# First stage of a two-request encoder layer: the sample's modulation products and the rotary tables moved from GpSimd to VectorE

## The chip, the cores and the metric

The kernel runs on one core of a Trainium2 chip. The core has five engines that work side by side, each through its own instruction stream in a fixed order: TensorE (PE in the profile, with its weight loads as PEld), VectorE (DVE), ScalarE (ACT), GpSimd (POOL) and SyncE (SP), which here issues most of the DMA transfers. The engines wait for each other through semaphores. The metric is the device time of one execution in microseconds (us); lower is better. The profile is that of one execution.

## The reference, cut to what matters

One encoder layer is applied to two requests that share all weights: a prompt of 512 tokens and a sample of 1,024 tokens, each with 1,024 channels, in float32. For each of them:

```
mod = (silu(c) @ w_ada + b_ada)             # 6 x 1024: shift, scale, gate for mixer and MLP
h   = rmsnorm(x, g_pre_mix) * (1 + scale_a) + shift_a
q, k, v, u = split(h @ w_in)                # 512 + 128 + 128 + 512 columns
q, k = rope(rmsnorm(q, g_q)), rope(rmsnorm(k, g_k))
a   = attention(q, k, v)                    # 8 heads, 2 key/value heads, bidirectional
p   = multiscale_pool(u)                    # 4 groups, windows 2, 4, 8, 16
x   = x + gate_a * rmsnorm(concat(a, p) @ w_out, g_post_mix)
h   = rmsnorm(x, g_pre_mlp) * (1 + scale_m) + shift_m
x   = x + gate_m * rmsnorm(relu(h @ w_ff1)**2 @ w_ff2, g_post_mlp)
```

The change concerns the first two lines, `mod` and `h`, and the tables of the rotary embedding `rope`: cosines and sines, multiplied by the gains g_q and g_k. `silu(c)` is one vector of 1,024 numbers for each request, so `mod` is a matrix-vector product with a matrix of 1,024 by 6,144. Two of its six parts, shift_a and scale_a, have to be there before the first projection `h @ w_in` can begin.

## The kernel before, in words

Activations lie transposed: channels on the 128 partitions in eight blocks, tokens along the free dimension. The weights w_ada come as 48 tiles of 128 output channels by 1,024 inputs, 512 KB each. A product of such a tile with silu(c), which `make_cb` has spread over all partitions (`cb0` for the prompt, `cb1` for the sample), summed along the free dimension, gives 128 numbers of `mod`. `gemv_part` (L224) does product and sum in one VectorE instruction (L225) and writes the sum into a column of `mod`. `mod_mix` (L228) then adds the bias (L231) and forms (1 + scale) times the norm's gain (L232) for one block of 128 channels.

The first stage is `in_proj_p` (L479). It loads the prompt's eight blocks of x (`hp`), sums their squares (L495 to L499) and turns them into a reciprocal root for each token by `norm_vec` (small VectorE steps at L164 to L168, then PE at L177 and ACT at L180). Then comes a loop over eight blocks k of channels (L509). Each turn
- loads two tiles of w_ada, `jb = k` for the shift and `jb = 8 + k` for the scale, into a ring of seven buffers (tag `ga`, L512 and L513), and computes the prompt's part of both on VectorE (L515);
- loads the block's weights `w`, which have a buffer for each k (L519, L520);
- calls `mod_mix(0, k)`, scales hp[k] by the root on VectorE (L522), and applies scale and shift on ScalarE (L523);
- runs seven matmuls that add block k into seven PSUM banks (L526). The profile counts two matmuls for each of these;
- computes the sample's part of the same two tiles. For k below 6 the product is done by GpSimd (L530) and the sum by ScalarE one turn later (`sums_late`, L503 to L507, called at L524 behind the turn's L523). For k = 6 and 7 both are one instruction on VectorE (L533, which is L225 in the profile).

A w_ada tile is free for the next load once the sample's part has read it. After the loop the PSUM banks are copied out and three more blocks of the projection are computed with the same input (L545 to L557). The sample's `mod_mix(1, k)` is called in the next stage, by `make_h` (L351 to L353).

`setup_rest` (L297) loads edge_t, wp, the gains `gt` and the cosines and sines `cs`, scales one half of the gains on VectorE (L302), and forms the rotary tables `tabs` with ten GpSimd operations on 128 by 256 elements (L311 to L315). It is called in one go after 20 steps of `in_proj_p` (L1224). A step is one `yield`, one of the seven matmuls; so this point lies near the end of turn k = 2. From there `weave` (L26) runs the rest of `in_proj_p` and, at 0.32 steps to each of its steps, `pre_norm` (L322): eight loads of the sample's x (512 KB each, L327, two buffers), ScalarE's squares (L328), and the sample's norm.

The order of each engine's stream is set by a scheduler that follows the order in which the program names the instructions, but may put one that is ready earlier. Waits for a buffer stay in the stream: an engine, or SP's queue, that meets such a wait stands still with all that is behind it. `tc.keep_in_program_order(ins)` pins an instruction behind the one named just before it on the same engine.

Of the kernel before, what the change touches and what calls it, by code (L numbers as in the profile page):

```python
# [11 lines left out]
AF = mybir.ActivationFunctionType  # L12
AL = mybir.AluOpType
# [12 lines left out]
def weave(fg, bgs):  # L26

    credit = [0.0] * len(bgs)
    for _ in fg:
        for i, (bg, rate) in enumerate(bgs):  # L30
            credit[i] += rate
            while credit[i] >= 1.0:
                credit[i] -= 1.0
                next(bg, None)
# [7 lines left out]
def chain(*gs):  # L42
    for g in gs:
        yield from g
# [3 lines left out]
def hymba_encoder_layer(ctx, tc, xp, xs, ns_, vec, gqk, rope, edge, ident_in, w_ada_c,  # L48
                        w_in_k, w_in, w_pool, w_out, w_ff1, w_ff2, yp, ys):
    nc = tc.nc  # L50
# [51 lines left out]
    mod = const.tile([128, 48, 2], F32, name="mod")  # L102
# [121 lines left out]
    def gemv_part(c, jb, r, cb, out):  # L224
        return nc.vector.tensor_tensor_reduce(out=out, in0=r, in1=cb, op0=AL.mult, op1=AL.add,  # L225
                                              scale=1.0, scalar=0.0, accum_out=mod[:, jb, c:c + 1])
# [65 lines left out]
    tabs = inp.tile([128, 4, 8, 64], F32, name="tabs")  # L292
# [4 lines left out]
    def setup_rest():  # L297
        dma(edge_t, edge)
        dma(wp.rearrange("p g d -> p (g d)"), w_pool)
        gt = tmp("gt", "y")  # L300
        dma(gt[:, 0:128], gqk.partition_broadcast(128))
        nc.vector.tensor_scalar(gt[:, 0:64], gt[:, 0:64], 0.125, None, op0=AL.mult)  # L302
        cst = tmp("cs", "t2")
        dma(cst, rope)
        cs = cst.rearrange("p (a b d) -> p a b d", a=2, b=8)

        def gb(lo):
            return gt[:, lo:lo + 32].unsqueeze(1).to_broadcast([128, 8, 32])
        for qk in range(2):
            o = 64 * qk  # L310
            nc.gpsimd.tensor_tensor(tabs[:, 2 * qk, :, 0:32], cs[:, 0], gb(o), AL.mult)  # L311
            nc.gpsimd.tensor_tensor(tabs[:, 2 * qk, :, 32:64], cs[:, 0], gb(o + 32), AL.mult)
            nc.gpsimd.tensor_scalar(tabs[:, 2 * qk + 1, :, 0:32], cs[:, 1], -1.0, None, op0=AL.mult)
            nc.gpsimd.tensor_tensor(tabs[:, 2 * qk + 1, :, 0:32], tabs[:, 2 * qk + 1, :, 0:32], gb(o + 32), AL.mult)
            nc.gpsimd.tensor_tensor(tabs[:, 2 * qk + 1, :, 32:64], cs[:, 1], gb(o), AL.mult)  # L315

    R_t = {}
    h_t = {}
# [108 lines left out]
    def u_evac(ps, g):  # L427
        u = pq.tile([128, 8 + 512 + 8], F32, name=f"up{g}")
        nc.gpsimd.memset(u[:, 0:8], 0.0)
        nc.gpsimd.memset(u[:, 520:528], 0.0)  # L430
        u_t[g] = u
        nc.scalar.activation(out=u[:, 8:520], in_=ps, func=AF.Copy)
# [46 lines left out]
    def in_proj_p():  # L479


        make_cb(0, cb0, ps_t, "t")
        make_cb(1, cb1, ps_t, "t")
        pss = [mm_tile() for _ in range(2)]
        pss += [ps_t.tile([128, 512], F32, tag="t", name="tb") for _ in range(2)]
        pss += [s2[:, 0:512], s2[:, 512:1024], ps_x.tile([128, 512], F32, tag="x", name="xb")]
        hp = []
        ss = st_p.tile([128, 512], F32, tag="ss", name="ss")
        for k in range(KB):
            t = pd.tile([128, 512], F32, name=f"hp{k}")  # L490
            dma(t, xp[k])
            hp.append(t)
        for k in range(KB):
            if k == 0:
                nc.scalar.activation(out=ss, in_=hp[k], func=AF.Square)  # L495
            else:
                sq = st_p.tile([128, 512], F32, tag="sq", name="sq")
                nc.scalar.activation(out=sq, in_=hp[k], func=AF.Square)
                nc.vector.tensor_tensor(ss, ss, sq, AL.add)  # L499
        R = norm_vec([ss])  # L500
        late = []

        def sums_late():  # L503
            while late:
                jb, r = late.pop(0)
                tc.keep_in_program_order(
                    nc.scalar.activation(out=r, in_=r, func=AF.Copy, accum_out=mod[:, jb, 1:2]))  # L507

        for k in range(KB):  # L509
            g = []  # L510
            for jb in (k, 8 + k):
                r = pa.tile([128, 1024], F32, tag="ga", name="ga", bufs=7)  # L512
                dma(r, w_ada_c[jb])  # L513
                junk = inp.tile([128, 1024], BF16, tag="j", name="junk", bufs=1)
                ins = gemv_part(0, jb, r, cb0, junk)  # L515
                if k:
                    tc.keep_in_program_order(ins)
                g.append((jb, r))
            w = pb[k].tile([128, 7, 128], F32, name=f"pw{k}")  # L519
            dma(w.rearrange("p b m -> p (b m)"), w_in_k[k])  # L520
            mod_mix(0, k)
            nc.vector.tensor_tensor(hp[k], hp[k], R, AL.mult)  # L522
            nc.scalar.activation(out=hp[k], in_=hp[k], func=AF.Identity, bias=mod[:, k, 0:1], scale=a_mix[:, k, 0:1])  # L523
            sums_late()  # L524
            for i in range(7):
                nc.tensor.matmul(pss[i], lhsT=w[:, i, :], rhs=hp[k], start=(k == 0), stop=(k == KB - 1))  # L526
                yield
            for jb, r in g:
                if k < 6:
                    nc.gpsimd.tensor_tensor(r, r, cb1, AL.mult)  # L530
                    late.append((jb, r))
                else:
                    tc.keep_in_program_order(gemv_part(1, jb, r, cb1, r))  # L533
        sums_late()
        xs_ = {}
        for i in (2, 3, 0, 4, 5, 1):
            xs_[STRIPES[i]] = evac(pss[i], pq.tile([128, 512], F32, name=f"xp{i}"))
        u_evac(pss[6], 0)
        yield
        posts.append(qk_post(0, 0, xs_[4], 4))  # L540
        posts.append(qk_post(0, 0, xs_[0], 0))
        posts.append(v_post(0, 0, xs_[5]))
        posts.append(u_post(0, 0))
        rp = run_posts()
        for g in range(1, 4):  # L545
            w = pc[3 - g].tile([128, 8, 128], F32, name=f"pu{g}")
            dma(w, w_in[6 + g].rearrange("p k m -> p (k m)"))
            ps = mm_tile()
            for k in range(KB):
                nc.tensor.matmul(ps, lhsT=w[:, k, :], rhs=hp[k], start=(k == 0), stop=(k == KB - 1))  # L550
                if k % 2:
                    next(rp, None)
                yield
            u_evac(ps, g)
            posts.append(u_post(0, g))
        for b in (1, 2, 3):
            posts.append(qk_post(0, 0, xs_[b], b))  # L557
        rest.append(rp)
# [661 lines left out]
    cb1 = pa.tile([128, 1024], F32, name="cb1")  # L1220
    ip = in_proj_p()
    for _ in range(20):
        next(ip)
    setup_rest()  # L1224
    weave(ip, [(chain(pre_norm(0), pre_norm(1)), 0.32)])
    for z in (pb_close, pa_close, pc_close, pd_close):
        z()

# [205 lines left out]
```

## Time and profile before

| | |
|---|---|
| time, median of 3 runs | 1739.14 us (1735.07 to 1743.35) |
| the profiled execution | 1736.51 us, of which the span from first to last instruction is 1734.7 |
| PE busy | 1627.4 us, 94% of the span |
| DVE busy | 1279.3 us, 74% |
| ACT busy | 892.2 us, 51% |
| POOL busy | 153.2 us, 9% |
| chain that ended last | PE 70%, DVE 12%, DMA 10%, ACT 4% |
| mean granted PE clock | 0.976 |

Durations and times of start count from the first instruction. In the views, a line `L225 DVE ... out<-in x16` names the line of the code, the engine, the tile written and the tiles read, and the number of instructions. Square brackets behind an instruction give the engine's idle time just before it and what ended it. A row of the waits reads: engine and instruction that waited, `<-` what it waited for, then total us, times and the longest. `SPq` is SP's queue of DMA issues; the length of an entry there includes its wait for a buffer.

The stage in question runs from about 5 us, when the first tile of w_ada is issued, to about 96 us, when PE goes on to the remaining blocks of the prompt's projection.

### The profile page before, as it was taken

Reading aid. Unit: us, or ns where it says so; the run is one execution under the profiler, and the core shown is the slowest. Engines: PE = TensorE matmul, PEld = TensorE weight load, DVE = VectorE, ACT = ScalarE, POOL = GpSimd, SP = SyncE. Lnnn points to the kernel's source line nnn. Section 1 sums busy time; section 2 is a strip of 40 time slices with the busy share of each in tenths; the row PEclk is TensorE's granted clock in tenths of the full one; section 3 lists DMA queues with packets and bytes.
Section 4 is the critical chain, followed back from the end, with each engine's and each line's share of the span. In section 5 each row is a group of like instructions: output and inputs, shape, how many; then the busy total and the mean of one; then the engine's idle time right before and its main releaser. Section 6 shows DMA issues by size and latency. Waiting matters only on the chain.

```text
span 1734.7 us, 21886 instructions
## 1 busy us (share of the span) xinstructions
PE 1627.4 (94%) x7676; PEld 1303.1 (75%) x7676; DVE 1279.3 (74%) x2151; ACT 892.2 (51%) x1444; POOL 153.2 (9%) x127
## 2 busy tenths in 40 slices
PE   6798999889998999999998999999999989999995
PEld 3357887678887888888886677788888768888875
DVE  7797887878766786666645577888876476868767
ACT  3465655468655555555433456744445554444432
POOL 4501000201100100101012200000000000000014
PEclk7899999999999999999998999999999999999997
DMA  6555566833555453332334766566653656344324
GB/s 235 206 194 171 152 188 216 258 96 108 184 168 169 161 178 122 98 113 86 95 100 143 231 215 213 171 242 218 227 210 127 213 180 194 128 146 142 109 77 146
DMA packets 150110, 287.44 MB, mean 166 GB/s; under 512 B 14960, under 2 KB 56176, under 8 KB 150000
## 3 DMA queue, kind: packets, MB, share of 16 engines
q1 hardware_dynamic: 125552, 258.25, 45.8%
q10 hardware_dynamic: 24448, 27.80, 5.2%
q8 instruction: 61, 1.00, 0.2%
q14 instruction: 49, 0.40, 0.1%
HBM read 223.07 MB, written 61.34 MB: 164 GB/s over the span
## 4 chain that ended last, share of the span: by engine, by line
PE 70%; DVE 12%; DMA 10%; ACT 4%; issue 3%; POOL 1%; SPq 1%; DVEq 0%; POOLq 0%; ACTq 0%
PE pa L834 17%; PE mm L834 9%; PE mm L157 8%; PE mm L156 8%; PE mm L155 8%; PE pc L834 5%; DMA raw<-in_w_ada_c 4%; PE s L612 3%; PE pT L631 3%; PE x L645 2%; PE x L644 2%; DMA raw<-in_w_ff 2%; DVE wl L136 1%; DVE raw L225 1%; DVE junk L225 1%
## 5 line engine op out<-in xcount | busy, mean ns | idle before, releaser
L155 PE MATMUL mm<-fh,wh 128*128 128x512 f32 x448 | 185.0, 414 | 11.1 <-ACT fh L708 8.3
L156 PE MATMUL mm<-fl,wh 128*128 128x512 f32 x448 | 180.4, 404 | 2.8 <-DVE fl L709 2.8
L157 PE MATMUL mm<-fh,wl 128*128 128x512 f32 x448 | 179.3, 401 | 0.9 <-DVE wl L136 0.9
L135 ACT ACTIVATE wh<-raw 128x1024 fp32r<-128x1024 f32 (+2 forms) x106 | 105.2, 994 | 119.8 <-PE mm L156 82.5
L136 DVE TENSOR_TENSOR wl<-raw,wh 128x1024 fp32r<-128x1024 f32 (+2 forms) x106 | 125.2, 1182 | 51.6 <-ACT wh L135 51.5
L834 PE MATMUL pa<-fo,wh 128*128 128x512 f32 x448 | 138.9, 391 | 0.7 <-ACT x L970 0.7
L635 DVE TENSOR_TENSOR pl<-pT,ph 128x512 fp32r<-128x512 f32 x160 | 108.2, 685 | 26.5 <-ACT ph L634 25.7
L619 ACT ACTIVATE p<-s,amx 128x1024 f32<-128x1024 f32 (+1 forms) x96 | 93.1, 970 | 59.6 <-DVE amx L617 55.5
L617 DVE TENSOR_REDUCE amx<-s 128x1 f32<-128x1024 f32 (+1 forms) x96 | 100.0, 1041 | 31.4 <-PE s L612 30.9
L634 ACT ACTIVATE ph<-pT 128x512 fp32r<-128x512 f32 x160 | 94.2, 594 | 38.9 <-PE pT L631 33.2
L834 PE MATMUL mm<-fo,wh 128*128 128x512 f32 x336 | 106.2, 398 | 4.0 <-ACT wh L840 4.0
L155 PEld LDWEIGHTS mm<-fh,wh 128*128 128x128 f32 x448 | 85.5, 192 | 29.8 <-ACT fh L708 10.1
L155 PE MATMUL mm<-hA,wh 128*128 128x512 f32 x256 | 106.0, 415 | 0.0
L156 PEld LDWEIGHTS mm<-fl,wh 128*128 128x128 f32 x448 | 86.1, 192 | 22.8 <-DVE fl L709 6.0
L631 PE MATMUL pT<-ident,p 128*128 128x128 f32 x640 | 95.4, 273 | 7.6 <-ACT p L622 3.5
L157 PEld LDWEIGHTS mm<-fh,wl 128*128 128x128 f32 x448 | 86.0, 192 | 21.0 <-DVE wl L136 1.8
L157 PE MATMUL mm<-hA,wl 128*128 128x512 f32 x256 | 100.6, 393 | 0.0
L156 PE MATMUL mm<-hA,wh 128*128 128x512 f32 x256 | 100.5, 393 | 0.0
L612 PE MATMUL s<-kst,q 128*128 128x512 f32 x320 | 92.3, 402 | 7.8 <-ACT p L619 4.3
L631 PEld LDWEIGHTS pT<-ident,p 128*128 128x128 f32 x640 | 77.6, 140 | 28.6 <-ACT p L622 6.1
L834 PEld LDWEIGHTS pa<-fo,wh 128*128 128x128 f32 x448 | 84.0, 188 | 19.5 <-ACT x L970 1.1
L834 PE MATMUL pa<-fo,wl 128*128 128x512 f32 x224 | 87.6, 391 | 0.0
(288 smaller groups left out, 3918.0 us busy)
## 6 DMA issues: line engine op xcount, KB each, us to landing
raw<-in_w_ff SPq DMA_DIRECT2D x56, 512.0 KB, 3.8
f_d<-x SPq DMA_DIRECT2D x98, 256.0 KB, 2.9
raw<-f_d SPq DMA_DIRECT2D x98, 256.0 KB, 3.0
raw<-in_w_ada_c SPq DMA_DIRECT2D x40, 512.0 KB, 4.0
g<-in_w_ada_c SPq DMA_DIRECT2D x24, 512.0 KB, 4.3
q<-q_d SPq DMA_DIRECT2D x96, 128.0 KB, 3.2
raw<-in_w_out SPq DMA_DIRECT2D x24, 512.0 KB, 4.4
rawx<-in_w_ff SPq DMA_DIRECT2D x20, 512.0 KB, 4.0
```

What stands on the lines that cost most here:

```text
L135: nc.scalar.activation(out=fh, in_=r[:, :n], func=AF.Copy)
L136: nc.vector.tensor_tensor(fl, r[:, :n], fh.bitcast(F32), AL.subtract)
L155: nc.tensor.matmul(ps, lhsT=wh[:, k, :], rhs=ah, start=(i == 0), stop=False)
L156: nc.tensor.matmul(ps, lhsT=wh[:, k, :], rhs=al, start=False, stop=False)
L157: nc.tensor.matmul(ps, lhsT=wl[:, k, :], rhs=ah, start=False, stop=(i == len(ks) - 1))
L612: nc.tensor.matmul(s[:, f * 512:(f + 1) * 512], lhsT=q[:, h, p, :], rhs=kst[c][:, kv, f * 512:(f + 1) * 512].bitcast(F32R), start=(p == 0) ...
L617: nc.vector.tensor_reduce(mx, s[:, :n], AX.X, AL.max, negate=True)
L619: nc.scalar.activation(out=pr, in_=s[:, :n], func=AF.Exp, bias=mx, accum_out=den)
L631: nc.tensor.transpose(t[:, k, :], pr[:, (4 * f + k) * 128:(4 * f + k + 1) * 128], ident)
L634: nc.scalar.activation(out=hi, in_=t, func=AF.Copy)
L635: nc.vector.tensor_tensor(lo, t, hi.bitcast(F32), AL.subtract)
L834: nc.tensor.matmul(ps, lhsT=x[:, k, :], rhs=y, start=start and k == i == 0, stop=k == n - 1 and i == 2, skip_group_check=not start)
```

## The change

The sample's products in the first stage are all done by `gemv_part` on VectorE, product and sum in one instruction. `late` now holds the tiles whose sample part is still to do, and `sample_part(4)`, called behind the turn's L523, works it down to four tiles: in turn k the two tiles of block k - 2. The last four follow after the loop with `sample_part(0)`, behind the copies out of PSUM. The GpSimd products and ScalarE's sums are gone from this stage. All sample parts are pinned.

`setup_rest` becomes a generator that is woven in at 0.13 steps for each step of `in_proj_p`, in three pieces: the loads and the scaling of `gt` (after 8 further steps, so at the end of turn 3), the four table operations for q (after 16), and the four for k (after 24). They run on VectorE, and the two GpSimd steps for the negated sine are one instruction now.

```diff
--- before.py
+++ after.py
@@ -306,13 +306,15 @@
 
         def gb(lo):
             return gt[:, lo:lo + 32].unsqueeze(1).to_broadcast([128, 8, 32])
+        yield
         for qk in range(2):
             o = 64 * qk
-            nc.gpsimd.tensor_tensor(tabs[:, 2 * qk, :, 0:32], cs[:, 0], gb(o), AL.mult)
-            nc.gpsimd.tensor_tensor(tabs[:, 2 * qk, :, 32:64], cs[:, 0], gb(o + 32), AL.mult)
-            nc.gpsimd.tensor_scalar(tabs[:, 2 * qk + 1, :, 0:32], cs[:, 1], -1.0, None, op0=AL.mult)
-            nc.gpsimd.tensor_tensor(tabs[:, 2 * qk + 1, :, 0:32], tabs[:, 2 * qk + 1, :, 0:32], gb(o + 32), AL.mult)
-            nc.gpsimd.tensor_tensor(tabs[:, 2 * qk + 1, :, 32:64], cs[:, 1], gb(o), AL.mult)
+            nc.vector.tensor_tensor(tabs[:, 2 * qk, :, 0:32], cs[:, 0], gb(o), AL.mult)
+            nc.vector.tensor_tensor(tabs[:, 2 * qk, :, 32:64], cs[:, 0], gb(o + 32), AL.mult)
+            nc.vector.scalar_tensor_tensor(tabs[:, 2 * qk + 1, :, 0:32], cs[:, 1], -1.0, gb(o + 32),
+                                           op0=AL.mult, op1=AL.mult)
+            nc.vector.tensor_tensor(tabs[:, 2 * qk + 1, :, 32:64], cs[:, 1], gb(o), AL.mult)
+            yield
 
     R_t = {}
     h_t = {}
@@ -500,14 +502,13 @@
         R = norm_vec([ss])
         late = []
 
-        def sums_late():
-            while late:
+        def sample_part(lag):
+
+            while len(late) > lag:
                 jb, r = late.pop(0)
-                tc.keep_in_program_order(
-                    nc.scalar.activation(out=r, in_=r, func=AF.Copy, accum_out=mod[:, jb, 1:2]))
+                tc.keep_in_program_order(gemv_part(1, jb, r, cb1, r))
 
         for k in range(KB):
-            g = []
             for jb in (k, 8 + k):
                 r = pa.tile([128, 1024], F32, tag="ga", name="ga", bufs=7)
                 dma(r, w_ada_c[jb])
@@ -515,27 +516,21 @@
                 ins = gemv_part(0, jb, r, cb0, junk)
                 if k:
                     tc.keep_in_program_order(ins)
-                g.append((jb, r))
+                late.append((jb, r))
             w = pb[k].tile([128, 7, 128], F32, name=f"pw{k}")
             dma(w.rearrange("p b m -> p (b m)"), w_in_k[k])
             mod_mix(0, k)
             nc.vector.tensor_tensor(hp[k], hp[k], R, AL.mult)
             nc.scalar.activation(out=hp[k], in_=hp[k], func=AF.Identity, bias=mod[:, k, 0:1], scale=a_mix[:, k, 0:1])
-            sums_late()
+            sample_part(4)
             for i in range(7):
                 nc.tensor.matmul(pss[i], lhsT=w[:, i, :], rhs=hp[k], start=(k == 0), stop=(k == KB - 1))
                 yield
-            for jb, r in g:
-                if k < 6:
-                    nc.gpsimd.tensor_tensor(r, r, cb1, AL.mult)
-                    late.append((jb, r))
-                else:
-                    tc.keep_in_program_order(gemv_part(1, jb, r, cb1, r))
-        sums_late()
         xs_ = {}
         for i in (2, 3, 0, 4, 5, 1):
             xs_[STRIPES[i]] = evac(pss[i], pq.tile([128, 512], F32, name=f"xp{i}"))
         u_evac(pss[6], 0)
+        sample_part(0)
         yield
         posts.append(qk_post(0, 0, xs_[4], 4))
         posts.append(qk_post(0, 0, xs_[0], 0))
@@ -1221,8 +1216,7 @@
     ip = in_proj_p()
     for _ in range(20):
         next(ip)
-    setup_rest()
-    weave(ip, [(chain(pre_norm(0), pre_norm(1)), 0.32)])
+    weave(ip, [(setup_rest(), 0.13), (chain(pre_norm(0), pre_norm(1)), 0.32)])
     for z in (pb_close, pa_close, pc_close, pd_close):
         z()
 
```

## The prediction, made before the result was known

> **What bounds the kernel now.** I read the page first, then busy time by stretch, then who waited for whom in the first 105 us, then the time lines of TensorE (PE), VectorE (DVE) and GpSimd (POOL) in that stretch, and last the groups, the tile views of mod and ga and the DMA issues. The page gives the span:
>
> ```profile
> span 1734.7 us, 21886 instructions
> ```
>
> The execution as a whole took 1736.51 us, 2.63 below the median of 1739.14. What this change can tell from no change is about 0.5%, or 8.7 us. Busy time by stretch (columns: length, PE, weight load, DVE, ACT, POOL, granted PE clock, DMA share, GB/s):
>
> ```profile
> 10.00:20.00 10.00, 4.68 (x20) 3.80 (x18) 8.49 (x13) 2.79 (x6) 4.56 (x2) 0.50 1.03 414
> 25.97:96.46 70.49, 57.33 (x128) 25.35 (x129) 55.38 (x97) 31.55 (x56) 35.58 (x20) 0.90 0.59 211
> 96.46:119.20 22.74, 22.74 (x69) 10.93 (x67) 22.74 (x61) 16.22 (x27) 0.00 (x0) 1.00 0.40 118
> ```
>
> The second row is the stage that changes: the eight blocks of the prompt's projection. PE idles 13 of its 70.5 us and POOL is in use for half of it. In the third row PE and DVE are both full and POOL is silent, so a gain in the stage has to reach both engines. The PE time line gives the price of a block:
>
> ```profile
> 25.97 3.78 PE L526 MATMUL mm<-hp,pw 128*128 128x512 f32 x4 [2.26 <-ACT hp L523]
> 35.05 1.98 PE L526 MATMUL mm<-hp,pw 128*128 128x512 f32 x4 [0.56 <-ACT hp L523]
> 63.84 3.78 PE L526 MATMUL mm<-hp,pw 128*128 128x512 f32 x4 [7.46 <-ACT hp L523]
> 83.51 1.90 PE L526 MATMUL mm<-hp,pw 128*128 128x512 f32 x4
> 89.54 1.90 PE L526 MATMUL mm<-hp,pw 128*128 128x512 f32 x4
> 92.14 1.05 PE L177 MATMUL nv_r<-ident,nv_rs 128*128 128x128 f32 x8
> 96.46 1.88 PE L550 MATMUL mm<-hp,pu 128*128 128x512 f32 x4
> ```
>
> A block that PE runs without a wait costs 89.54 - 83.51 = 6.03 us. The first costs 35.05 - 25.97 - 0.56 = 8.5, its first four at about half speed. Block 4 starts after 7.46 us of idling, again with 3.78 where a running PE shows 1.90. What PE waits for is the modulated input, and that in turn waits for DVE:
>
> ```profile
> ACT hp L523 <- DVE a_mix L232: 34.4, 6, 8.8
> PE mm L526 <- ACT hp L523: 15.4, 6, 7.5
> DVE mod L231 <- ACT ga L507: 7.8, 3, 3.0
> ```
>
> DVE is late for two reasons. One is the third of these waits: a small addition for the sample's scale and shift, in DVE's queue ahead of the prompt's next products, waits for the sums on ACT, which wait for POOL. The other shows when the time line of DVE (first fence) is laid beside POOL's (second):
>
> ```profile
> 15.29 1.29 DVE L164 TENSOR_SCALAR nv_rs<-nv_ms 128x4 int32<-128x4 int32 x1
> 17.82 2.32 DVE L167 SCALAR_TENSOR_TENSOR rs_t<-rs_t,nv_ms 128x4 f32<-128x4 f32 x1
> 20.57 0.16 DVE L167 SCALAR_TENSOR_TENSOR rs_t<-rs_t,nv_ms 128x4 f32<-128x4 f32 x1
> 24.38 0.69 DVE L522 TENSOR_TENSOR hp<-hp,nv_R 128x512 f32<-128x512 f32 x1 [2.86 <-ACT nv_R L180]
> 30.64 2.30 DVE L231 TENSOR_TENSOR mod<-mod,vt 128x2 f32<-128x2 f32 x1
> 92.80 0.16 DVE L232 SCALAR_TENSOR_TENSOR a_mix<-mod,vt 128x1 f32<-128x1 f32 x1
> 95.66 1.23 DVE L136 TENSOR_TENSOR wl<-raw,wh 128x1024 fp32r<-128x1024 f32 x1 [2.70 <-ACT wh L135]
> ```
>
> ```profile
> 17.79 2.34 POOL L530 TENSOR_TENSOR ga<-ga,cb 128x1024 f32<-128x1024 f32 x1 [1.24 <-DVE rs_t L166]
> 30.19 2.73 POOL L530 TENSOR_TENSOR ga<-ga,cb 128x1024 f32<-128x1024 f32 x1 [1.17 <-DVE mod L225]
> ```
>
> A two-element addition that starts at 30.64 ends at 32.94, within 0.02 of the end of the POOL product that began at 30.19 (32.92). The 2.32 us step at 17.82 ends at 20.14, the POOL product at 20.13. So DVE stands still until POOL is done. How much of it there is, by tile (min/median/max in ns) and by group (busy, mean ns):
>
> ```profile
> L231 DVE TENSOR_TENSOR mod<-mod,vt x16: 159/164/2300, 17.7 to 92.6; 128x2 f32<-128x2 f32 x16
> L232 DVE SCALAR_TENSOR_TENSOR a_mix<-mod,vt x16: 146/160/2268, 20.1 to 92.8; 128x1 f32<-128x1 f32 x16
> L225 DVE CUSTOM_DVE_ANT_0 junk<-ga,cb x16: 1211/1218/3383, 12.8 to 86.9; 128x1024 bf16<-128x1024 f32 x16
> ```
>
> ```profile
> L231 DVE TENSOR_TENSOR mod<-mod,vt 128x2 f32<-128x2 f32 x16 | 11.7, 732 | 8.0 <-ACT ga L507 7.8
> L232 DVE SCALAR_TENSOR_TENSOR a_mix<-mod,vt 128x1 f32<-128x1 f32 x16 | 9.9, 622 | 0.3
> L225 DVE CUSTOM_DVE_ANT_0 junk<-ga,cb 128x1024 bf16<-128x1024 f32 x16 | 23.8, 1487 | 3.0 <-DMA ga<-in_w_ada_c 2.9
> L225 DVE CUSTOM_DVE_ANT_0 ga<-ga,cb 128x1024 f32<-128x1024 f32 x4 | 4.8, 1220 | 0.0
> L530 POOL TENSOR_TENSOR ga<-ga,cb 128x1024 f32<-128x1024 f32 x12 | 30.6, 2560 | 31.7 <-DVE mod L225 27.5 <-issue 1.7 <-DVE a_mix L232 1.2
> L507 ACT ACTIVATE ga<-ga 128x1024 f32<-128x1024 f32 x12 | 12.5, 1040 | 0.0
> L398 DVE TENSOR_TENSOR t<-y,tabs 128x256 f32<-128x256 f32 x2 | 0.9, 429 | 0.0
> L523 ACT ACTIVATE hp<-hp,mod,a_mix 128x512 f32<-128x512 f32 x8 | 6.5, 811 | 35.2 <-DVE a_mix L232 34.4 <-DVE hp L522 0.8
> ```
>
> Mean less median, times 16, is 9.1 us for L231, 7.4 for L232 and 4.3 for L225: 20.8 us of DVE's 55.4 is standing still.
>
> **The change, term by term.** Work on DVE. Gone: the 20.8 us. Added: twelve products at 1.22 us (the four that DVE already does for the sample), 14.6; eight table operations at 0.43 (the nearest DVE row of that size, L398), 3.4. 55.4 - 20.8 + 14.6 + 3.4 = 52.6 us. The Trainium skill (SBUF — State Buffer, section "SBUF: two separate sides") describes the port pair that the two engines share as an exclusive lock which one of them holds for a whole instruction while the other blocks. The two ends above agree with it; read strictly, it would let DVE lose up to the whole of POOL's 30.6 us, and DVE's work afterwards would be as little as 42.8, where the rows say 52.6. I go by the rows. GpSimd's 30.6 us and ACT's 12.5 us of sums fall away; neither sets an end by itself, but with them the wait of 7.8 us goes, since product, sum and addition then follow each other on one engine.
>
> The start. Ahead of the first block lies the prompt's norm. Without POOL, L164 and L167 lose 1.29 - 0.16 and 2.32 - 0.16, together 3.3 us. The first scaling moves from 24.38 to 21.1, PE's first matmul from 25.97 to 22.7.
>
> If PE then never waits: 8.5 for the first block, seven at 6.03, and two insertions for the sample's norm (8 matmuls at L177), each 0.9 (the last block with one took 96.46 - 89.54 = 6.92). 22.7 + 8.5 + 42.2 + 1.8 = 75.2, instead of 96.46: 21.3 us earlier.
>
> Does DVE keep up? That hangs on the ring of seven weight tiles, for which the rows are, from SP's time line, the tile view and the DMA issues of the stretch:
>
> ```profile
> 16.85 0.33 SPq L304 DMA_DIRECT2D cs<-in_rope  x1
> 17.98 18.41 SPq L513 DMA_DIRECT2D ga<-in_w_ada_c x2
> ```
>
> ```profile
> DMA to landing us min/median/max: 3.6/6.9/9.9
> ```
>
> ```profile
> g<-in_w_ada_c SPq DMA_DIRECT2D x1, 512.0 KB, 3.8
> gt<-in_gqk SPq DMA_DIRECT2D x1, 64.0 KB, 7.2
> ```
>
> Now SP stands still for 18 us in the middle of block 3's two loads, until the first tile comes free. After the change, the second tile of block k reuses the slot that the first sample product of block k-3 frees, and that product stands in iteration k-1. The first such product comes behind three scalings (0.69 each), four prompt products and two pairs of additions (0.4 a pair: the last L232 starts 0.2 after the last L231): 21.1 + 2.1 + 4.9 + 0.8 = 28.9. From there each block is a loop: one sample product (1.22), the landing of the freed load, one prompt product (1.22), the additions (0.4). An uncrowded load lands in 3.8, so 6.64, say 6.8 us with issue. Block 7's additions come at 28.9 + 5 x 6.8 = 62.9, its scaled input (ACT, 0.81) at 63.7; PE wants it at 75.2 - 6.9 = 68.3. So PE has cover of 4.6 us.
>
> What eats of that cover. The four setup loads moved from SP's place ahead of the blocked load to a place behind it and behind two loads for the sample's norm. The scaling of gt (L302) goes with them, and the first product of block 4 is pinned behind it. Freed at 28.9 + 1.2, with six issues of 0.33 or a little more ahead of gt, the queue reaches it near 33, and at 7.2 it lands near 40; the product would otherwise run near 38. 2 us, inside the cover. Nobody else waits: rotary tables, edge_t and wp are first read after the stage. A table group of 1.7 us sits in blocks 5 and 6 ahead of pinned products; DVE's wait for the landing (3.8, less two products of 1.22, 1.4 idle) takes up most. The cover gone, each would delay PE one for one.
>
> The hand-over. DVE now ends the stage at 92.96 (92.80 + 0.16) and idles until 95.66, when the next stage's work reaches it. For the saving to be whole, DVE must be done by 95.66 - 21.3 = 74.4. Its work from the first scaling on is 52.6 and the 1.6 between 24.38 and 25.97, so without any wait it ends at 21.1 + 54.2 = 75.3, late by 0.9. If none of the 1.4 us in five blocks were filled, it would be late by 7.9. I take 0.5 us a block unfilled, nearer the first since tables, additions and norm steps are there to fill it: late by 3.4, charged in full, because the next stage shows DVE without a gap.
>
> Sum: 21.3 - 3.4 = 17.9 us. 1736.51 becomes 1718.6 for a profiled execution, the median 1739.14 becomes 1721.2, say **1721 us**. Bounds on the forecast's own terms: 21.3 - 7.9 = 13.4 (1726) and 21.3 - 0.9 = 20.4 (1719); an altered order later in the kernel, which no row can price, I allow 5 us more on the good side (1714).
>
> **Rivals.** (1) Crowded loads: the landing is 6.9, the median of the tile view, not 3.8. The loop is 9.7, block 7's additions at 28.9 + 48.7 = 77.6, PE done at 77.6 + 0.8 + 6.0 = 84.4; DVE still has six products and three pairs of additions, to 86.1 against the 83.6 at which the next stage wants it. 96.46 - 84.4 - 2.5 = 9.6: 1730. For: a block's loads with two for the norm are 2,496 KB, 6.2 us at 414 GB/s. Against: nothing is ahead of a freed load when SP has stood still.
>
> (2) No gain: DVE's long instructions are its own. Then it has 55.4 + 18 = 73.4 us for a stage of 70.5, and the time stays, 1739 to 1742. The Trainium skill (Perfetto Trace Analysis, section "Optimizing Scalar/DVE Operations") speaks for this side: with a saturated DVE, moving work off it may pay; here work moves onto it at 79% busy. Against it: two ends that meet within 0.02 us, and no such length once POOL falls silent.
>
> (3) Slower: the ring becomes the bound. Now a slot's second tile is requested late only once; after, in each of five blocks. At the 9.9 us that the slowest tile took, the loop is 12.7, block 7's additions come at 28.9 + 63.7 = 92.6, PE ends at 99.4 and DVE hands over 2.5 late: 5.4 us lost, 1744.5. It decides from a landing of 8.8 us on; more than 0.5% slower takes 10.5.
>
> **How the numbers follow.** Forecast 0.64; a better order later on 0.05; rival 1 0.18, of which 0.13 over the bound of 8.7 us; rival 2 0.08; rival 3 0.05. Faster 0.64 + 0.05 + 0.13 = 0.82; same 0.05 + 0.08 = 0.13; slower, with rival 3 whole, 0.05. The range runs from 1714 to 1732: the good side's bound, and rival 1 with some 2 us for the spread between executions (the median and the profiled one differ by 2.63). It leaves out rivals 2 and 3, 0.13.
>
> **What would show it.** Right: no L231 or L232 over 0.3 us before 80 us; PE's first L526 at about 22.7 and its first L550 at about 75, with waits of under 2 us between; DVE's first L136 near 77; SP's stop before block 3's second load ending near 30. Wrong: landings of ga over 6 us in blocks 3 to 7 (rival 1, or 3 above 8.8), or a first L550 near 75 with PE idle from 75 to 130, which would mean that DVE takes the saving back.

## The result and the profile after

| | before | after |
|---|---|---|
| median of 11 runs each, taken side by side | 1737.28 us (1734.13 to 1743.35) | 1725.09 us (1723.94 to 1731.43) |
| ratio, 95% interval | | 0.9934 (0.9921 to 0.9948) |
| profiled execution; its span | 1736.51; 1734.7 | 1725.06; 1723.1 |
| PE / DVE / ACT / POOL busy | 1627.4 / 1279.3 / 892.2 / 153.2 | 1625.1 / 1267.0 / 880.1 / 111.2 |

The kernel is faster by 12.2 us, 0.7%. It was forecast to save 17.9. The lines moved a little: the stage's matmuls are L527 (they were L526), the next blocks of the projection L545 (L550), ScalarE's scale and shift L524 (L523), VectorE's scaling L523 (L522), the posts' transposes L374 (L372). A post is the normalising and rotating of a stripe of queries or keys (`qk_post`); PE transposes for it.

The PE time line after (start, length, instruction; in brackets the idle time ahead and what ended it):

```profile
23.65 3.78 PE L527 MATMUL mm<-hp,pw 128*128 128x512 f32 x4 [2.26 <-ACT hp L524]
32.51 1.88 PE L527 MATMUL mm<-hp,pw 128*128 128x512 f32 x4
50.53 1.88 PE L527 MATMUL mm<-hp,pw 128*128 128x512 f32 x4
69.90 1.88 PE L527 MATMUL mm<-hp,pw 128*128 128x512 f32 x4
76.36 1.88 PE L545 MATMUL mm<-hp,pu 128*128 128x512 f32 x4
99.11 0.48 PE L155 MATMUL mm<-hh,wh 128*128 128x512 f32 x1
125.17 1.09 PE L374 MATMUL nat<-ident,xp 128*128 128x128 f32 x4 [9.28 <-DVE rs_t L167]
```

Between 23.65 and 76.36 no matmul has a bracket: PE runs the eight blocks without a wait and starts the next work 20.1 us earlier than before (96.46). The last row is new in size: PE idles 9.28 us ahead of one post's transposes, where the kernel before idled 3.64:

```profile
119.23 0.48 PE L155 MATMUL mm<-hh,wh 128*128 128x512 f32 x1
144.81 1.09 PE L372 MATMUL nat<-ident,xp 128*128 128x128 f32 x4 [3.64 <-DVE rs_t L167]
```

The DVE time line after, and the modulation tile's view (min/median/max in ns):

```profile
22.05 0.69 DVE L523 TENSOR_TENSOR hp<-hp,nv_R 128x512 f32<-128x512 f32 x1 [2.86 <-ACT nv_R L180]
39.24 0.18 DVE L302 TENSOR_SCALAR gt<-gt 128x64 f32<-128x64 f32 x1
63.61 0.17 DVE L332 TENSOR_SCALAR pn_ms<-pn_ms 128x4 f32<-128x4 f32 x1 [3.88 <-ACT raw L330]
67.05 0.16 DVE L231 TENSOR_TENSOR mod<-mod,vt 128x2 f32<-128x2 f32 x1
72.57 0.28 DVE L232 SCALAR_TENSOR_TENSOR a_mix<-mod,vt 128x1 f32<-128x1 f32 x2
75.55 1.23 DVE L136 TENSOR_TENSOR wl<-raw,wh 128x1024 fp32r<-128x1024 f32 x1 [2.70 <-ACT wh L135]
```

```profile
L231 DVE TENSOR_TENSOR mod<-mod,vt x16: 144/151/164, 17.6 to 72.5; 128x2 f32<-128x2 f32 x16
L232 DVE SCALAR_TENSOR_TENSOR a_mix<-mod,vt x16: 140/146/160, 17.8 to 72.7; 128x1 f32<-128x1 f32 x16
```

No small addition stands still any more (0.164 us at most, before 2.3). DVE ends the stage at 72.57 + 0.28 = 72.85 and then idles 2.70 us for the next weights, exactly as before: nothing was handed over late.

So the first stage gained 20 us, and the whole 12. Busy time by stretch finds the difference. After, from the sample's first matmul (L155 on `hh`) to its first on `hA` (the next part of the layer), and from there to the last group of matmuls:

```profile
23.65:76.36 52.71, 52.71 (x129) 24.23 (x130) 45.85 (x129) 19.31 (x32) 0.00 (x0) 0.95 0.76 286
99.11:396.90 297.79, 269.00 (x1411) 216.49 (x1409) 237.22 (x540) 166.00 (x306) 25.37 (x17) 0.97 0.58 174
396.90:1706.80 1309.90, 1266.82 (x6011) 1039.06 (x6012) 940.42 (x1404) 668.69 (x1042) 80.28 (x70) 0.99 0.49 160
```

The same two stretches of the kernel before:

```profile
119.23:409.80 290.57, 269.63 (x1430) 218.75 (x1428) 238.44 (x544) 166.64 (x306) 24.90 (x17) 0.98 0.58 178
409.80:1718.40 1308.60, 1264.12 (x5996) 1036.74 (x5995) 938.58 (x1401) 666.52 (x1039) 82.55 (x70) 0.99 0.49 160
```

Up to the sample's first matmul 20.1 us are saved (119.23 - 99.11). The second stretch takes 297.79 us instead of 290.57 and gives 7.2 back; the last takes 1.3 more. 20.1 - 7.2 - 1.3 = 11.6 us. PE and DVE are busy in the second stretch for as long as before (269.00 and 269.63, 237.22 and 238.44), so the 7.2 us are idling of PE: 28.8 instead of 20.9. The longest waits of PE in that part are, after:

```profile
PE nat L374 <- DVE rs_t L167: 9.3, 1, 9.3
PE mm L155 <- ACT wh L135: 3.6, 1, 3.6
```

Before, the first of these was 3.6 and the second was not among the waits.

### The profile page after: what moved, and what is told of

It is laid out like the page before. It is cut to its first block, busy times and chain, and to the rows that moved or that the text cites. A ratio compares the mean times of both kernels' runs of the same rounds, so it can differ in the third digit from the quotient of the medians.

```text
span 1723.1 us, 21870 instructions
## 1 busy us (share of the span) xinstructions
PE 1625.1 (94%) x7676; PEld 1302.7 (76%) x7676; DVE 1267.0 (74%) x2183; ACT 880.1 (51%) x1420; POOL 111.2 (6%) x105
## 4 chain that ended last, share of the span: by engine, by line
PE 71%; DVE 10%; DMA 10%; ACT 4%; issue 3%; POOL 1%; SPq 0%; ACTq 0%; DVEq 0%; POOLq 0%
PE pa L829 16%; PE mm L829 10%; PE mm L156 8%; PE mm L157 8%; PE mm L155 8%; PE pc L829 5%; DMA raw<-in_w_ada_c 4%; PE s L607 3%; PE pT L626 3%; DMA raw<-in_w_ff 3%; PE x L640 2%; PE x L639 2%; DVE raw L225 1%; DVE wl L136 1%; PE mm L527 1%
## 5 line engine op out<-in xcount | busy, mean ns | idle before, releaser
L155 PE MATMUL mm<-fh,wh 128*128 128x512 f32 x448 | 185.0, 414 | 12.6 <-ACT fh L703 6.7
L156 PE MATMUL mm<-fl,wh 128*128 128x512 f32 x448 | 180.4, 404 | 3.1 <-DVE fl L704 3.1
L157 PE MATMUL mm<-fh,wl 128*128 128x512 f32 x448 | 179.4, 401 | 0.5 <-DVE wl L136 0.5
L155 PEld LDWEIGHTS mm<-fh,wh 128*128 128x128 f32 x448 | 86.0, 192 | 31.2 <-ACT fh L703 8.4
L629 ACT ACTIVATE ph<-pT 128x512 fp32r<-128x512 f32 x160 | 94.2, 593 | 26.4 <-PE pT L626 25.3
L155 PE MATMUL mm<-hA,wh 128*128 128x512 f32 x256 | 106.2, 416 | 0.7 <-ACT hA L220 0.7
L156 PEld LDWEIGHTS mm<-fl,wh 128*128 128x128 f32 x448 | 86.0, 192 | 23.6 <-DVE fl L704 6.7
L156 PE MATMUL mm<-hA,wh 128*128 128x512 f32 x256 | 100.8, 394 | 0.6 <-DVE hA L221 0.6
L157 PEld LDWEIGHTS mm<-fh,wl 128*128 128x128 f32 x448 | 85.8, 191 | 20.2 <-DVE wl L136 1.0
L157 PE MATMUL mm<-hA,wl 128*128 128x512 f32 x256 | 100.5, 393 | 0.0
```

The lines of the kernel that those rows point to most:

```text
L155: nc.tensor.matmul(ps, lhsT=wh[:, k, :], rhs=ah, start=(i == 0), stop=False)
L156: nc.tensor.matmul(ps, lhsT=wh[:, k, :], rhs=al, start=False, stop=False)
L157: nc.tensor.matmul(ps, lhsT=wl[:, k, :], rhs=ah, start=False, stop=(i == len(ks) - 1))
L629: nc.scalar.activation(out=hi, in_=t, func=AF.Copy)
```

## The experiments

The kernel of experiment n is called kernel n below. Three questions were open. Is the gain of the first stage really the end of DVE's standing still beside GpSimd (the lock theory), and which part of the change brings it? Is the loss in the second stretch a wait for buffers? After the change ScalarE waits there 2.80 and 2.69 us for the store of the pooled output `po` to leave buffers that it shares (before 0.30 and 2.50); this is theory A. Or is it the order in which the scheduler put the streams? In the kernel before, PE's stream holds 23 triples of sample matmuls (L155, L156, L157) ahead of that post's transposes, and after the change 16: the order theory. Ratios below are to the kernel before, run in the same job, that is, side by side on the same chip; between jobs, ratios compare better than times.

**1. The buffers of the pooled output.** The kernel after, with the prompt's `po` written over its input, so that ScalarE need not wait for the store:

```diff
-            po = st_p.tile([128, 512], F32, tag="sq", name="po")
+            po = st_p.tile([128, 512], F32, tag="sq", name="po") if c else mx
```

> The changed kernel, with one thing more: the prompt's four pooled results (po) are written over the inputs that their matmuls have just read, instead of into the two buffers that they share with the squares of the query/key posts. So ScalarE no longer waits for the stores p_d<-po (in the changed kernel 2.80 us before its third po and 2.69 before the squares at 118.12). Theory A (the 8.5 us that are saved in the first stage and lost by the end go in the chain store p_d, ScalarE's squares, VectorE's roots, the third post's transposes, behind which PE's next blocks stand): the squares come 4 to 5 us earlier against the first sample matmul, and the time falls by about 4.4 us to some 1721. Theory B (the loss is one of order: the transposes stand too early in PE's stream, whatever they wait for): here they stand after 13 triples of sample matmuls instead of 16, PE still waits 5 to 9 us there, and the time stays within 2 us of 1725.

Measured: 1732.03 us (1728.99 to 1735.12), ratio 0.9974 (0.9961 to 0.9987). The order moved as well, to 13 triples. PE's longest waits behind the first stage:

```profile
PE nat L374 <- DVE y L402: 7.0, 2, 6.2
PE nat L374 <- DVE qrs L164: 4.8, 1, 4.8
```

ScalarE's waits for the store are gone, and the kernel is 7 us slower than the one after. The order theory's number for this run is missed too: it was not neutral but a third, worse order. Since the order moved as well, this run alone doesn't settle theory A. The traces of other kernels do. ScalarE's waits for the store in the kernel after (first fence) and in kernel 10 (second fence), which has 23 triples:

```profile
ACT po L475 <- DMA p_d<-po: 2.8, 1, 2.8
ACT sqh L384 <- DMA p_d<-po: 2.7, 1, 2.7
```

```profile
ACT sqh L384 <- DMA p_d<-po: 3.2, 1, 3.2
ACT po L475 <- DMA p_d<-po: 2.6, 1, 2.6
```

The waits are as long there, and kernel 10 is faster than the kernel after by 7 us in the medians (ratios 0.9879 and 0.9934). Theory A falls.

**2. The products alone.** The kernel after with `setup_rest` as it was: in one go, the tables on GpSimd.

```diff
-            nc.vector.tensor_tensor(tabs[:, 2 * qk, :, 0:32], cs[:, 0], gb(o), AL.mult)
...
+            nc.gpsimd.tensor_tensor(tabs[:, 2 * qk, :, 0:32], cs[:, 0], gb(o), AL.mult)
...
-    weave(ip, [(setup_rest(), 0.13), (chain(pre_norm(0), pre_norm(1)), 0.32)])
+    setup_rest()
+    weave(ip, [(chain(pre_norm(0), pre_norm(1)), 0.32)])
```

> One part of the change alone: the sample's products on VectorE two blocks behind, but setup and rotary tables as before (in one go after 20 steps, on GpSimd). From the second stage on its instruction streams are almost those of the kernel before: the third post's transposes stand behind 23 triples of sample matmuls, not 16. Ten table operations on GpSimd hold VectorE for 2 to 5 us inside the first stage, which PE's cover takes. Both theories: first matmul on the remaining prompt blocks at 76 to 78 us, as with the whole change. Theory B (order): the wait before the transposes is back to 3 to 5 us, nearly the whole saving reaches the end, 1718 to 1720. Theory A (stores p_d are slow because the shifted loads crowd them): they still take over 5 us, the wait is over 8 us, and the time is 1725 to 1727.

Measured: 1720.89 us (1716.9 to 1725.76), ratio 0.9912 (0.9894 to 0.993): by the medians faster than the whole change, with less of it, though the two intervals overlap; a little above what was expected. The order is back at 23 triples. In the first stage PE has two waits that it lacks after the whole change:

```profile
49.60 1.98 PE L525 MATMUL mm<-hp,pw 128*128 128x512 f32 x4 [1.84 <-ACT hp L522]
57.44 0.46 PE L177 MATMUL nv_r<-ident,nv_rs 128*128 128x128 f32 x2 [1.56 <-DVE nv_rs L168]
```

So the stage is 3.4 us longer (56.1 from its first matmul, 21.23, to the next blocks, 77.33) and the kernel is not slower for it: what the whole change loses, it loses later.

**3. The tables alone.** The kernel before with the tables on VectorE, woven in at 0.13.

```diff
-            nc.gpsimd.tensor_tensor(tabs[:, 2 * qk, :, 0:32], cs[:, 0], gb(o), AL.mult)
...
+            nc.vector.tensor_tensor(tabs[:, 2 * qk, :, 0:32], cs[:, 0], gb(o), AL.mult)
...
-    setup_rest()
-    weave(ip, [(chain(pre_norm(0), pre_norm(1)), 0.32)])
+    weave(ip, [(setup_rest(), 0.13), (chain(pre_norm(0), pre_norm(1)), 0.32)])
```

> The other part alone: rotary tables on VectorE, woven in at 0.13, with the sample's products on GpSimd and ScalarE as before. Lock theory (VectorE stands still while a GpSimd product runs): ten table operations (8.6 us on GpSimd) no longer stand before the products of block 3, but all twelve products still hold VectorE; the short operations at L231 and L232 keep lengths over 2 us. The stage ends 3 to 6 us earlier than before, the time is 1731 to 1735. Rival (GpSimd's tables were the main burden, the products are not): the stage ends over 12 us earlier and the time is below 1728.

Measured: 1735.82 us (1731.54 to 1740.73), ratio 0.9999 (0.9988 to 1.001). The next blocks start at 95.99 (before 96.46), and the longest small addition is still 2.302 us. The 3 to 6 us that I expected did not come: a miss. While the products stay on GpSimd the tables are worth nothing that shows.

**4. GpSimd given work that nobody reads.** The kernel after with twelve products into a spare tile:

```diff
+        spare = pd.tile([128, 1024], F32, name="spare")
+        for _ in range(12):
+            nc.gpsimd.tensor_tensor(spare, cb0, cb1, AL.mult)
```

> The changed kernel plus twelve GpSimd products of 128 by 1024 elements that nobody reads (cb0 times cb1 into a spare tile), free to run back to back after the two vectors are there. They add work that the reference does not have. Lock theory: they run from about 15 to 45 us; VectorE's operations with two inputs in that time are as long as a product (2 to 3.4 us) whatever they are, about 20 us of standing still; the first matmul comes 3 to 8 us later, PE waits in blocks 1 to 4, and the next stage starts 8 to 16 us later than at 76.36: 1733 to 1741. Rival (VectorE's long operations were waits for the products' results): nothing waits for these, no operation of VectorE gets longer, and the time stays at 1725.

Measured: 1750.97 us (1748.01 to 1753.28), ratio 1.0084 (1.0068 to 1.0099). GpSimd's time line, VectorE's beside it, and PE's first matmuls of the stage:

```profile
13.05 32.84 POOL L506 TENSOR_TENSOR spare<-cb,cb 128x1024 f32<-128x1024 f32 x12 [11.97 <-ACT cb L276]
```

```profile
14.07 1.91 DVE L164 TENSOR_SCALAR nv_rs<-nv_ms 128x4 int32<-128x4 int32 x1
17.03 2.29 DVE L166 TENSOR_TENSOR rs_t<-nv_rs 128x4 f32<-128x4 f32 x1
19.43 2.30 DVE L232 SCALAR_TENSOR_TENSOR a_mix<-mod,vt 128x1 f32<-128x1 f32 x1
34.29 3.37 DVE L225 CUSTOM_DVE_ANT_0 junk<-ga,cb 128x1024 bf16<-128x1024 f32 x1
```

```profile
35.27 3.78 PE L530 MATMUL mm<-hp,pw 128*128 128x512 f32 x4 [3.88 <-ACT hp L527]
```

Nothing waits for the spare tile, and the streams of PE keep the order after (16 triples). The long additions and the 3.37 us product are back while GpSimd works. The first matmul starts at 35.27 (after: 23.65), the next blocks at 94.99 (76.36): 18.6 us of the stage are lost to work whose result nobody reads. The lock theory's mechanism is shown; I had put its price too low, at 8 to 16 us for the stage and at most 1741 for the whole, and the kernel lost 26. DVE is busy 1292.5 us in place of 1267.0 with the same 2183 instructions, so 25.5 of GpSimd's 32.0 us (12 of 2.665 each) were DVE standing still.

**5. The order of the kernel before, restored.** The kernel after with only the rate changed at which the setup is woven in:

```diff
-    weave(ip, [(setup_rest(), 0.13), (chain(pre_norm(0), pre_norm(1)), 0.32)])
+    weave(ip, [(setup_rest(), 0.1), (chain(pre_norm(0), pre_norm(1)), 0.32)])
```

> The changed kernel with one constant altered: setup is woven in at 0.10 steps instead of 0.13, so its three pieces come after 10, 20 and 30 further steps. All work stays on VectorE. But from the second stage on the instruction streams are those of the kernel before again (the third post's transposes behind 23 triples of sample matmuls, not 16). Theory B (what the second stage takes back is a matter of this order): next stage starts at 75 to 77.5 us as with the change, the wait before the transposes is 5 to 6 us, and the time is 1718 to 1721, 4 to 7 us below the change. Rival (the loss comes from the shift itself, as loads and stores meet differently): 1724 to 1727.

With 0.1 the transposes stand behind 23 triples again. More than that: from the sample's first matmul on, all five engines run the same operations on the same tiles, by the names in the traces, in the same order as in the kernel before, and so they do in kernels 3 and 9. Measured: 1714.69 us (1712.68 to 1716.07), ratio 0.9873 (0.9853 to 0.9893), 10.4 us faster than the kernel after, where I had expected 4 to 7. Its PE time line and its stretches:

```profile
124.44 0.86 PE L374 MATMUL nat<-ident,xp 128*128 128x128 f32 x4 [3.60 <-DVE rs_t L167]
```

```profile
98.88:386.30 287.42, 269.11 (x1430) 218.18 (x1428) 237.77 (x543) 166.57 (x306) 25.57 (x17) 0.99 0.59 179
386.30:1697.30 1311.00, 1268.43 (x5997) 1041.09 (x5995) 938.29 (x1402) 667.54 (x1039) 81.32 (x70) 0.98 0.49 159
```

The sample's first matmul starts as early as after the change (98.88 and 99.11), and now all of the gain arrives: 409.8 - 386.3 = 23.5 us at the end of the second stretch, of which the last one gives 2.4 back (1311.0 - 1308.6). The second stretch is 297.79 - 287.42 = 10.4 us shorter than after, with the same work on PE and DVE: as much as the medians differ. At the transposes one sees how the order does it. VectorE frees them at almost the same moment (125.17 and 124.44). With 16 triples ahead PE has run out of work at 125.17 - 9.28 = 115.9; with 23 it has seven triples more to run (0.68 us each, 4.8 in all) and idles 3.60.

**6. The order after, given to the kernel before.** The kernel before with the rate of `pre_norm` changed:

```diff
-    weave(ip, [(chain(pre_norm(0), pre_norm(1)), 0.32)])
+    weave(ip, [(chain(pre_norm(0), pre_norm(1)), 0.3)])
```

> The kernel before with one constant altered: the sample's norm is woven in at 0.30 steps instead of 0.32. All products stay on GpSimd and ScalarE, the first stage stays as long as it was (next stage at 95 to 98 us), but the second stage's streams are those of the changed kernel (third post's transposes behind 16 triples). Theory B: the wait before the transposes grows from 3.6 to 8 to 10 us, and the time rises by 3 to 7 us over the kernel before. Rival: no difference to the kernel before, within 2 us.

Measured: 1750.42 us (1749.13 to 1752.92), ratio 1.0083 (1.0067 to 1.01). It has 16 triples ahead of the transposes, PE's stream from the sample's first matmul on is that of the kernel after but for a few matmuls, and both of that kernel's waits are there:

```profile
PE nat L372 <- DVE rs_t L167: 9.0, 1, 9.0
PE mm L155 <- ACT wh L135: 3.7, 1, 3.7
```

```profile
119.79:419.20 299.41, 268.89 (x1411) 215.63 (x1409) 239.49 (x539) 166.18 (x306) 25.27 (x17) 0.98 0.58 173
```

The order alone costs the kernel before 14.6 us, 8.8 of them in the second stretch (299.41 - 290.57) and 3.4 behind it; I expected less. Order against order, the change is worth 1735.82 - 1714.69 = 21.1 us with 23 triples and 1750.42 - 1725.09 = 25.3 with 16 (the last two from different jobs).

**7. Another order.** The kernel after with the setup woven in at 0.2, which gives 21 triples:

```diff
-    weave(ip, [(setup_rest(), 0.13), (chain(pre_norm(0), pre_norm(1)), 0.32)])
+    weave(ip, [(setup_rest(), 0.2), (chain(pre_norm(0), pre_norm(1)), 0.32)])
```

> The changed kernel with setup woven in at 0.20: the same work, next stage at 75 to 78 us, but a third order of the later streams (transposes behind 21 triples). It shows how far a time moves by order alone. Theory B: between the change and the order of before, 1720 to 1726. Rival (order is of no weight): 1725 within 1.

Measured: 1731.3 us (1727.34 to 1734.21), ratio 0.9973 (0.996 to 0.9986). A miss: 21 is not between 16 and 23 in time, but behind both, though the first stage ends early (74.92). PE's waits:

```profile
PE nat L374 <- DVE rs_t L167: 5.7, 1, 5.7
PE nat L374 <- DVE aden L615: 5.4, 2, 5.0
```

A later post's transposes, too, now come too early. So the count of triples at one place names an order; it doesn't price it.

**8. and 9. The lag of two blocks.** The kernel after with the sample's products in the same turn, and kernel 5 with them one block behind:

```diff
-            sample_part(4)
+            sample_part(0)
```

> The changed kernel with sample_part(0) instead of (4): the sample's products of a block follow in the same turn, not two blocks behind. Its later order is nearly that of the run with setup at 0.20, so it is to be compared with that one. If the two-block lag is what keeps PE fed: PE waits before several blocks, 1 to 4 us each, and the next stage starts 4 to 12 us later. If PE's cover takes it (VectorE needs about 6.1 us a block and PE 6.0, and a tile comes free earlier): the next stage starts within 3 us of the other run's, and the time is within 3 us of it.

```diff
-            sample_part(4)
+            sample_part(2)
```

> The run with setup at 0.10 and sample_part(2): the sample's products one block behind the prompt's, not two. PE's, ScalarE's and SP's streams are that run's but for a few lines. If the lag is worth nothing because PE's cover takes it: within 2 us of 1714.7, next stage at 75 to 77.5. If the two blocks matter: PE waits 1 to 3 us before some blocks and the time is 1718 to 1722.

Measured: 1731.9 us (1727.92 to 1734.84), ratio 0.9973 (0.9962 to 0.9985), in the order of kernel 7 (21 triples, its two long waits 6.0 and 5.0), whose 1731.3 it equals in the same job; and 1716.76 us (1712.56 to 1722.36), ratio 0.9873 (0.9851 to 0.9895), with the order and the ratio of kernel 5. The lag itself is worth nothing that shows.

**10. The good order by another rate.** The kernel after with the setup at 0.08, again 23 triples:

```diff
-    weave(ip, [(setup_rest(), 0.13), (chain(pre_norm(0), pre_norm(1)), 0.32)])
+    weave(ip, [(setup_rest(), 0.08), (chain(pre_norm(0), pre_norm(1)), 0.32)])
```

> The changed kernel with setup at 0.08: a further constant at which the later streams are those of the kernel before (transposes behind 23 triples). Theory B: the time follows the order, not the constant, 1713 to 1718. Rival (1714.7 at 0.10 is a lucky constant of the first stage): 1720 or more.

Measured: 1717.9 us (1715.78 to 1721.8), ratio 0.9879 (0.9858 to 0.99), the time of kernel 5 within the intervals. The order is not quite the same one, though: here and in kernel 2 the streams differ from kernel 5's at a few places. That the rate itself is not the cause, kernel 3 shows better: it has the change's rate of 0.13 and the streams of the kernel before, and its second stretch takes 406.40 - 118.75 = 287.7 us.

**11. No GpSimd in the sample's inputs either.** Kernel 5 with the last GpSimd steps of `make_h` on VectorE:

```diff
-                     eng=nc.gpsimd if hf and k > 3 else nc.vector)
+                     eng=nc.vector)
```

> The run with setup at 0.10, and the four scalings of make_h that GpSimd still does (5 us, just ahead of the third post) on VectorE as well, so no GpSimd work is left before attention. The order of the later streams becomes a fifth one (transposes behind 27 triples, later than in any run so far). Lock theory with theory B: VectorE's roots are not held up, the wait before the transposes is under 3.6 us, 1710 to 1715. If only the order counts and this one happens to be worse: 1720 to 1732.

Measured: 1722.98 us (1721.63 to 1728.04), ratio 0.9912 (0.9892 to 0.9931), slower than kernel 5: missed. Here 27 triples stand ahead of the transposes, and their wait is all but gone (0.97 us), yet PE waits elsewhere:

```profile
PE s L607 <- ACT p L614: 3.9, 4, 1.7
PE mm L156 <- DVE fl L704: 2.6, 2, 1.4
PE s L607 <- DMA q<-q_d: 2.5, 1, 2.5
```

The stretch to the first `hA` takes 391.6 - 96.24 = 295.4 us, near that after (297.8). The place of these transposes alone doesn't decide.

Over all runs, the profiled second stretch sorts by order. Where the streams are identical it takes 287.4 us (kernel 5), 287.7 (3), 288.6 (9) and 290.6 (the kernel before); with 23 triples and a few places altered 291.7 (10) and 293.8 (2). In each of the seven others it takes 295.3 to 304.1. The spread of 3.2 us among identical streams shows how closely one profiled execution can be read.

## Why the prediction was right, and where it missed

The direction, the mechanism of the first stage and the range held; the size was 5.7 us too large.

- **The lock, 20.8 us.** Right in kind, too small in size (next item), and rival 2 (DVE's long instructions are its own) falls: they vanish without GpSimd (0.164 us at most) and come back with unread GpSimd work (kernel 4). The rule of the Trainium skill (Perfetto Trace Analysis, "Optimizing Scalar/DVE Operations") that moving work off a saturated DVE may make sense would by itself have pointed the wrong way here, since part of DVE's busy time was waiting. I cited half of that paragraph: it goes on to warn that moving work between GpSimd and VectorE might not help, as they share a port. The standing still in kernel 4 is in line with that warning, though here the move from GpSimd to VectorE did help. The strict reading of the lock in the Trainium skill (SBUF — State Buffer, "SBUF: two separate sides") is nearer than I thought: in kernel 4 DVE lost 25.5 us to 32.0 of GpSimd.
- **DVE's work of 52.6 us.** Too high: 45.85. For the comparison each instruction is counted with the time by which it lengthens DVE's busy time. The three rows that I had counted then fell by 22.6 us, not 20.8. Lines that I hadn't counted fell by 3.3 more: scalings of `hp` (0.5), steps of the roots (1.0), and the sample's norm (1.8), two steps of 1044 ns on average that take 165 now:

```profile
L330 DVE TENSOR_SCALAR pn_ms<-pn_ms 128x4 f32<-128x4 f32 x2 | 2.1, 1044 | 0.6 <-ACT raw L328 0.6
```

```profile
L332 DVE TENSOR_SCALAR pn_ms<-pn_ms 128x4 f32<-128x4 f32 x2 | 0.3, 165 | 3.9 <-ACT raw L330 3.9
```

The twelve added products cost 13.6 us where I counted 14.6, and the tables 2.7 for 3.4, since in the profile DVE's instructions overlap a little: the next one begins 1.15 us after a product of 1.22, and 0.34 after a table step of 0.41.
- **The start, 22.7.** 23.65. The squares' last sum, ahead of all that the change touches, came 1.3 us later in this execution (13.49, before 12.23). With the products on VectorE the first matmul began between 21.2 (kernel 2) and 23.7, kernel 4 apart.
- **The stage, 75.2 - 22.7 = 52.5.** Right: 76.36 - 23.65 = 52.71, without a wait.
- **The ring.** The forecast of SP's stop, gt and the loads was right in place. From SP's queue after:

```profile
28.70 0.33 SPq L514 DMA_DIRECT2D ga<-in_w_ada_c  x1
54.56 1.37 SPq L329 DMA_DIRECT2D raw<-in_ns_  x2
56.02 0.86 SPq L514 DMA_DIRECT2D ga<-in_w_ada_c  x2
```

The stop for block 3's second tile ended at 28.70 (near 30), and gt was scaled at 39.24 (near 40) without delay. But my sign for rivals 1 and 3 appeared without its price. From 28 to 60 us the tiles took 6.5 us to land (median of nine), over the 6 that was to mean a loss:

```profile
ga<-in_w_ada_c SPq DMA_DIRECT2D x9, 512.0 KB, 6.5
```

The loop that I built on the landing wasn't the pace. From 30 to 62 us SP stood still for buffers of the sample's x, and hardly for a weight tile:

```profile
SPq L329 <- ACT raw L330: 14.3, 5, 5.9
SPq L514 <- DVE mod L225: 1.8, 2, 1.5
```

Block 7's tiles were issued at 56.02, behind loads of the sample's x that SP reached only at 54.56, landed at 61.94 and 63.21, and their products came behind a step of the sample's norm (63.61) that idled 3.88 us for ScalarE's squares of that x. The additions of block 7 came at 67.05, not 62.9, its scaled input at 68.25, and PE took it at 69.90: a cover of 1.65 us where I had 4.6. It was enough.
- **The hand-over, "late by 3.4, charged in full".** This step failed. DVE was done at 72.85, not 77.8, and the loss was nothing. DVE idled 4.2 us on its way, more than the 2.5 that I allowed, but it had 6.75 us less to do.
- **"An altered order later in the kernel, which no row can price, I allow 5 us more on the good side".** This is the step that made the difference. The order did change, and on the bad side: 10.4 us against the order of the kernel before (kernel 5), all of it in the second stretch. The sum as it came out is 20.1 - 7.2 - 1.3; in the old order it is 21.1 (kernel 5), about what the first stage was to bring by itself, 21.3. That the total fell near the forecast is in part two errors that lean against each other. The sign that I gave for a loss, PE idle between 75 and 130, did appear, but not for the reason given: DVE had no more work there than in kernel 5 (237.22 and 237.77).

**Left open.** Of the 10.4 us, 5.7 show at the transposes (9.28 - 3.60) and 3.6 at the wait for the converted weights; both came with the 16-triple order in kernel 6 and the kernel after, but neither place was changed by itself. Nor was it tried why a rate of 0.13 tips the scheduler's order and 0.1 doesn't. What the tables add to the products is open too. Kernel 2 is 6.2 us slower than kernel 5 (1720.89 - 1714.69, different jobs), but its next blocks start only 1.2 us later (77.33 and 76.12), while its second stretch, in an order with a few places altered, is 6.4 longer; and the interval of kernel 2 overlaps that of kernel 10.

## What to carry to other kernels

Before work is called too much for VectorE, look for short instructions with long maxima that end with a GpSimd instruction: their excess is not work, and moving GpSimd's share onto VectorE can make VectorE less busy. After any edit under a scheduler, compare the order of each engine's stream with that of before, and where it changed, time the edit in both orders: here the order was worth 10 to 17 us (kernel 7 is 16.6 behind kernel 5), the edit 21 to 25. Follow a gain to the end by milestones (first matmul of each part); the stretch in which it shrinks, with equal busy times, is where the order has to be read.

## What the runs showed of the hardware

- GpSimd products and VectorE held each other up. In kernel 4 six of the twelve products took 2.34 us, with only small VectorE steps in between; the other six took 2.67 to 3.27, and beside each of them VectorE did a product or a scaling. The shortest in the kernel before took 2.33.
- Even an integer step on 128 by 4 elements with one tensor input stood still beside them: 1.91 us (L164 in kernel 4), 0.17 without GpSimd.
- Twelve GpSimd products whose results nobody reads delayed PE's first matmul by 11.6 us (35.27 - 23.65) and the whole kernel by 26.
